# One encoder block on one core: where W_out's upper rows are split, when the second FFN's kept operands are made and loaded, and when norm 2's vectors come

## The chip, the cores and the metric

The kernel runs on one core of a Trainium2 chip, alone. The metric is the time of one execution on the device, in microseconds (us). Five engines work side by side, each through its own instructions in order: PE (matrix products), DVE (elementwise), ACT (elementwise and functions), POOL (elementwise, and it issues DMAs that store) and SP, which issues the DMAs that load.

## The reference

One block with 1024 tokens and a width of 1024, in float32:

```python
x = layer_norm(DN_ALPHA * x + 0.5 * swiglu(x, ffn1_w_gate[l], ffn1_w_up[l], ffn1_w_down[l]), ln1_g[l], ln1_b[l])
z = x @ w_in[l]
fox = forgetting_attention(q, k, v, fg).reshape(bsz, seq, FOX_W)      # 8 heads of 64
u = causal_depthwise_conv(z[..., LX_OFF:LX_OFF + LRU_W], conv_w[l], conv_b[l])
rec = rg_lru(u, rg_wa[l], rg_ba[l], rg_wx[l], rg_bx[l], lru_lambda[l])
lru = jax.nn.gelu(z[..., LG_OFF:LG_OFF + LRU_W]) * rec
mix = jnp.concatenate([fox, lru], axis=-1) @ w_out[l]                 # (1024, 1024) @ (1024, 1024)
x = layer_norm(DN_ALPHA * x + mix, ln2_g[l], ln2_b[l])
x = layer_norm(DN_ALPHA * x + 0.5 * swiglu(x, ffn2_w_gate[l], ffn2_w_up[l], ffn2_w_down[l]), ln3_g[l], ln3_b[l])
```

`swiglu(x, g, u, d)` is `(silu(x @ g) * (x @ u)) @ d` with an inner width of 4096. `layer_norm` is `(x - mean) * rsqrt(var + eps) * g + b` along the 1024 columns.

## The kernel before

**Products.** Every float32 operand is split in two: `hi`, its rounding to a shorter format, cast on ACT, and `lo`, the rest, subtracted on DVE. A product of 128x128 by 128x512 is three matmuls, `hi hi`, `hi lo` and `lo hi` (L163 to L165). Most work on ACT and DVE is this splitting.

**FFN1's first half** (`gate_up`). The 4096 inner columns go in 16 pairs of 256. For each pair the gate and the up matrix, 1024x256 each (1 MB), are loaded raw, and each is multiplied with x by seven block products in place of eight (`one` to `seven`), which take sums and differences of the weights' quarters: L355 makes them on DVE, L349 and L350 split them. `seven` adds into the bank of `six`, and so waits for the copy L659 of it; `three` waits in the same way for L663. The operands of both matrices of a pair, 28 tiles, lie in a pool of 16 buffers (`ws`) that are given out in turn. The first pair of FFN1 (`first_pair`) has an order written out by hand for PE, DVE and ACT, since x has to be transposed and summed there first: L443 copies a transposed block out of its bank, L449 adds two blocks, and L385/L391 split. A scheduler orders all the rest.

**`prepare`** runs beside FFN1's pairs, as a generator: at the steps `two` and `five` of each matrix `next(steps)` does one piece of it. It makes the seven operands of FFN2's first pair ahead, from raw tiles of 128 KB (`aux`, two buffers) that SP loads: a subtraction on DVE, the split (L278 on ACT, L279 on DVE) into a `ws` buffer, and a store to `pre_d` that POOL issues (L285). After 28 such pieces come 16 more, which split rows 0 to 511 of W_out in the same way and store them to `wo_d` (L317).

**Attention.** 64 units, one for each head and tile of 128 queries, run at most three ahead of their use. Up to unit 36 or so the other half of W_out's product fills PE in between. Units 45 to 51 load the four parts of W_out's rows 0 to 511 from `wo_d` (`ready_out_w`, hi and lo of 512 KB each), and units 40, 50 and 52 load the mixed heads that were stored on the way (`mix_d`). Behind the last of them come norm 2's g and b (`load_gb`), and POOL negates g, so that the norm's chain for 1/sqrt(var) can give its negative.

**FFN2's first pair** (`ready_pair`) loads the kept operands from `pre_d`: twelve tiles into `ws` buffers, and t4 and t2 into the two raw buffers (L556); its remaining operands follow later.

Of the kernel before, what the change touches and what calls it, by code (L numbers as in the profile page):

```python
# [59 lines left out]
class Block:  # L60
# [127 lines left out]
    def load_gb(self, g, b, gb):  # L188

        for t, v in zip(gb, (g, b)):  # L190
            self.fetch(t, bass.AP(tensor=v.tensor, offset=v.offset, ap=[[0, P], [1, D]]))
        self.nc.gpsimd.tensor_scalar(gb[0], gb[0], -1.0, 1.0, op0=ALU.mult, op1=ALU.mult)
        self.gb = gb

    def layer_norm(self, i, done=None):
# [67 lines left out]
    def prepare(self, views, to_d, w_out, wsp, ap):  # L263
# [17 lines left out]

        for m, view in enumerate(views):
            for h in range(2):
                def out(n, src):
                    nc.gpsimd.dma_start(to_d[m, OPERANDS.index(n), h], f32(halves(src)))  # L285
# [4 lines left out]
                v.tensor_tensor(b, b, a, ALU.subtract)  # L290
                a = load(view, down, 1)
                yield
                out("t1", b)
                yield
                out("22", a)
                v.tensor_tensor(a, a, b, ALU.subtract)
                b = load(view, down, 0)
                yield
                out("t2", a)
                yield  # L300
                out("21", b)
                v.tensor_tensor(b, b, a, ALU.subtract)
                a = load(view, down, 1)
                yield
                out("t4", b)
                b = load(view, up, 1)
                v.tensor_tensor(a, a, b, ALU.subtract)
                yield
                out("t3", a)
                yield  # L310
        self.wo_d = self.dram.tile([FOX // P, P, 2, D], F32, name="wo_d")
        for f in range(FOX // P):
            for c in range(4):
                cols = slice(c * 2 * P, (c + 1) * 2 * P)
                a = raw()
                nc.sync.dma_start(a.rearrange("p k c -> p (k c)"), w_out[f * P:(f + 1) * P, cols])
                nc.gpsimd.dma_start(self.wo_d[f, :, :, cols], f32(halves(a)).rearrange("p (l k) c -> p l (k c)", l=2))  # L317
                yield
# [15 lines left out]
    def gate_up(self, wg, wu, h_d, rows, bank, tp, wsp, raws=None, later=None, aside=None, ready=None, steps=None):  # L334
# [211 lines left out]
        def ready_pair(g, u):  # L546
# [13 lines left out]
            for n in ("11", "21", "t1"):  # L560
                for m in both:
                    fetch(n, m, two_blocks())
            for n in ("t4", "t2"):
                r = self.rawp.tile([P, 4, 4, P], F32R, tag="raw", name=self.nm("raw"))
                for i, m in enumerate(both):
                    fetch(n, m, (r[:, 2 * i], r[:, 2 * i + 1]))
# [115 lines left out]
        for pair in range(FF // P // 2):  # L682
# [39 lines left out]
            for m in (gate, up):  # L722
# [391 lines left out]
    def ready_out_w(self):  # L1114

        for f in range(FOX // P):
            hl = tuple(self.wsp.tile([P, 4 * VW], F32R, tag="ws", name=self.nm("w"))[:, 0:D] for _ in range(2))
            for l in range(2):
                self.nc.sync.dma_start(f32(hl[l]), self.wo_d[f, :, l])
            yield hl  # L1120

    def attention(self, w_out, mixp, ln, normed):
# [7 lines left out]
        with self.pool("att_p", 3) as pp, self.pool("att_t", 1) as tp, self.pool("att_pt", 6) as ptp, self.pool("att_qk", 2, side="right") as qkp:  # L1130
# [92 lines left out]
            tiles, mix, w_fox, w_steps = [], [], [], self.ready_out_w()  # L1223
# [17 lines left out]
            for n in range(len(units) + AHEAD + 1):  # L1241
# [22 lines left out]
                if 45 <= n < 53 and n % 2:  # L1264
                    w_fox.append(next(w_steps))
                if n in MIXES:
                    mix.append(tuple(self.hp.tile([P, T], F32R, tag="h", name=self.nm("mix")) for _ in range(2)))
                    for l in range(2):
                        nc.sync.dma_start(f32(mix[-1][l]), mix_d[len(mix) - 1][l])
                    if len(mix) == 3:  # L1270
# [144 lines left out]
```

## Time and profile before

| | |
|---|---|
| median of 3 runs | 2322.07 us (2321.42 to 2322.68) |
| the profiled execution, its time | 2323.19 us |
| the profiled execution, its span | 2321.5 us |
| mean granted clock of PE | 0.997 |
| DMA, mean over the span | 139 GB/s |
| read from and written to HBM | 226.81 MB, 94.40 MB |

The trace shows for each instruction its engine, its line, its start and duration, and what ended the idle time ahead of it. In a timeline row the columns are start, duration, engine, line, operation, the tile written, the tiles read, and in brackets the idle time of the engine ahead of it and its releaser. A row of waits has the sum, the number of times and the longest. A row of windows has the stretch and its length; busy time and count of PE, of its weight loads, of DVE, ACT and POOL; the granted clock of PE (1.00 is full speed); the share of the DMA engines; GB/s. Matmuls of 512 columns start 0.23 us apart and are shown 0.39 long, since they overlap.

### The profile page before, as it was taken

To read this page: it belongs to the slowest core of one execution; us is meant where nothing else is said; L and a number is where in the kernel's file an instruction comes from. 1 tells how busy PE (TensorE), PEld (TensorE's weight loads), DVE (VectorE), ACT (ScalarE), POOL (GpSimd) and SP (SyncE) were. 2 spreads that over 40 slices of the span, in tenths; PEclk is the share of its full clock that TensorE was granted. 3 is DMA by queue.
4 is the path that set the end of the run, shared out by engine and by line. 5 is a ranking of instruction groups with operands and counts; after the bars stand their busy time and mean duration, and the time that the engine had idled before them with its cause. 6 is when DMAs were issued, how large, how long until landed. Compare 5 with 4: busy or idle time off the path is not lost.

```text
span 2321.5 us, 28560 instructions
## 1 busy us (share of the span) xinstructions
PE 2298.7 (99%) x10705; PEld 1914.1 (82%) x10705; DVE 1635.6 (70%) x2521; ACT 1019.1 (44%) x1623; POOL 227.8 (10%) x388
## 2 busy tenths in 40 slices
PE   8999999999999999999999999999999999999998
PEld 7888888888888888888898788888888888888887
DVE  7867666666467788866667899565656665577886
ACT  5443434343344345453556755334333333344341
POOL 0121111100000000111133210000000000000000
PEclk9999999999999999999999999999999999999999
DMA  4444444433276433233274934232323232564542
GB/s 150 141 141 145 139 147 141 146 113 125 101 259 234 147 127 109 75 92 110 91 218 126 283 137 141 86 118 89 122 93 123 87 118 87 195 244 168 182 144 73
DMA packets 194444, 323.08 MB, mean 139 GB/s; under 512 B 10033, under 2 KB 115825, under 8 KB 194305
## 3 DMA queue, kind: packets, MB, share of 16 engines
q1 hardware_dynamic: 167712, 230.74, 30.9%
q0 software_dynamic: 26592, 90.51, 9.9%
q8 instruction: 84, 1.38, 0.3%
q14 instruction: 56, 0.45, 0.1%
HBM read 226.81 MB, written 94.40 MB: 138 GB/s over the span
## 4 chain that ended last, share of the span: by engine, by line
PE 81%; issue 10%; DVE 3%; DMA 3%; POOL 2%; ACT 1%; SPq 0%; POOLq 0%; DVEq 0%; ACTq 0%
PE x L163 7%; PE x L164 7%; PE x L165 7%; PE s L165 6%; PE s L164 6%; PE s L163 6%; PE a L165 6%; PE a L164 6%; PE a L163 6%; PE b L163 6%; PE b L164 6%; PE b L165 6%; PE a L1200 1%; PE a L1179 1%; PE a L1049 1%
## 5 line engine op out<-in xcount | busy, mean ns | idle before, releaser
L349 ACT CAST ws<-t 128x512 fp32r<-128x512 f32 x240 | 148.9, 623 | 374.2 <-PE b L164 253.0
L349 ACT CAST ws<-raw 128x512 fp32r<-128x512 f32 x180 | 111.0, 622 | 239.3 <-PE x L164 237.3
L350 DVE TENSOR_TENSOR ws<-t,ws 128x512 fp32r<-128x512 f32 x240 | 164.3, 686 | 56.4 <-ACT ws L349 50.6
L350 DVE TENSOR_TENSOR ws<-raw,ws 128x512 fp32r<-128x512 f32 x180 | 123.3, 688 | 114.4 <-ACT ws L349 110.3
L164 PE MATMUL a<-ws,ws 128*128 128x512 f32 x512 | 199.8, 390 | 0.2
L163 PE MATMUL a<-ws,ws 128*128 128x512 f32 x512 | 199.3, 390 | 0.4 <-ACT row L672 0.4
L163 PE MATMUL b<-As,ws 128*128 128x512 f32 x512 | 199.4, 389 | 0.2 <-ACT row L663 0.2
L164 PE MATMUL b<-As,ws 128*128 128x512 f32 x512 | 199.3, 389 | 0.0
L165 PE MATMUL b<-As,ws 128*128 128x512 f32 x512 | 199.2, 389 | 0.0
L165 PE MATMUL a<-ws,ws 128*128 128x512 f32 x512 | 199.2, 389 | 0.0
L163 PE MATMUL x<-As,ws 128*128 128x512 f32 x504 | 196.6, 390 | 2.1 <-ACT row L659 2.0
L164 PE MATMUL x<-As,ws 128*128 128x512 f32 x504 | 196.1, 389 | 0.0
L165 PE MATMUL x<-As,ws 128*128 128x512 f32 x504 | 196.1, 389 | 0.0
L163 PE MATMUL x<-A,ws 128*128 128x512 f32 x496 | 193.3, 390 | 0.0
L165 PE MATMUL x<-A,ws 128*128 128x512 f32 x496 | 193.0, 389 | 0.0
L164 PE MATMUL x<-A,ws 128*128 128x512 f32 x496 | 193.0, 389 | 0.0
L772 ACT CAST ws<-raw 128x1024 fp32r<-128x1024 f32 x112 | 117.4, 1050 | 157.8 <-PE a L164 87.2
L775 DVE TENSOR_TENSOR ws<-raw,ws 128x1024 fp32r<-128x1024 f32 x112 | 136.6, 1220 | 53.0 <-ACT ws L772 52.6
L702 POOL DMA_DIRECT2D h_d<-row x96 | 68.9, 719 | 968.5 <-DVE row L696 928.4
L163 PE MATMUL s<-ws,ws 128*128 128x512 f32 x384 | 149.5, 389 | 0.0
L165 PE MATMUL s<-ws,ws 128*128 128x512 f32 x384 | 149.4, 389 | 0.0
L164 PE MATMUL s<-ws,ws 128*128 128x512 f32 x384 | 149.4, 389 | 0.0
(295 smaller groups left out, 5252.7 us busy)
## 6 DMA issues: line engine op xcount, KB each, us to landing
raw<-h_d SPq DMA_DIRECT2D x56, 1024.0 KB, 5.4
h_d<-row POOLq DMA_DIRECT2D x96, 512.0 KB, 3.5
wd<-in_ffn_w_down_dram SPq DMA_DIRECT2D x32, 1024.0 KB, 7.5
raw<-in_ffn_w_gate_dram SPq DMA_DIRECT2D x30, 1024.0 KB, 5.3
raw<-in_ffn_w_up_dram SPq DMA_DIRECT2D x30, 1024.0 KB, 5.3
h_d<-row POOLq DMA_DIRECT2D x32, 256.0 KB, 2.7
raw<-in_w_in_dram SPq DMA_DIRECT2D x16, 512.0 KB, 4.9
pre_d<-ws POOLq DMA_DIRECT2D x28, 256.0 KB, 2.7
```

What stands on the lines that cost most here:

```text
L163: mm(out, ah, bh, start=first, stop=False, skip_group_check=goes_on)
L164: mm(out, ah, bl, start=False, stop=False, skip_group_check=goes_on)
L165: mm(out, al, bh, start=False, stop=last, skip_group_check=goes_on)
L349: nc.scalar.copy(hi, src)
L350: v.tensor_tensor(lo, src, f32(hi), ALU.subtract)
L702: nc.gpsimd.dma_start(d[:, 2 * n:2 * n + 2], t.rearrange("p (r t) -> p r t", r=2))
L772: cast = nc.scalar.copy(hi, src)
L775: self.mark = v.tensor_tensor(lo, src, f32(hi), ALU.subtract)
L1049: nc.tensor.matmul(pa[:, 0:width], xh, wh[:, 0:width], start=k == 0, stop=False)
L1179: nc.tensor.transpose(pa[:, (j % 4) * P:(j % 4 + 1) * P], p[:, j * P:(j + 1) * P], self.ident)
L1200: mm(pv[:, ps], vt[:, j, :], pts[h, qt][j // 4][l][:, j % 4, ps], start=j == 0 and l == 0, stop=j == last and l == 1)
```

## The change

Rows 0 to 511 of W_out are loaded raw in attention and split there by `out_w`, as its other rows are already; the 16 pieces in `prepare`, `wo_d` and `ready_out_w` are gone. `prepare` advances once in a matrix, at `two`, and its loads are issued behind the newest raw weight load. The loads of FFN2's kept operands at the start of `ready_pair` are issued behind the last load of the mixed heads. Norm 2's g and b are loaded at unit 38. g is not negated any more, in all three norms: the chain has -0.5 for 0.5 and an addition for a subtraction.

```diff
-        self.nc.gpsimd.tensor_scalar(gb[0], gb[0], -1.0, 1.0, op0=ALU.mult, op1=ALU.mult)
...
-        v.tensor_scalar(w, mv[:, 1:2], EPS, 0.5, op0=ALU.add, op1=ALU.mult)
+        v.tensor_scalar(w, mv[:, 1:2], EPS, -0.5, op0=ALU.add, op1=ALU.mult)
...
-        v.scalar_tensor_tensor(y, w, 1.5, y, op0=ALU.subtract, op1=ALU.mult)
+        v.scalar_tensor_tensor(y, w, 1.5, y, op0=ALU.add, op1=ALU.mult)
...
                 a, b = load(view, up, 0), load(view, up, 1)
-                out("11", a)
-                v.tensor_tensor(b, b, a, ALU.subtract)
+                yield
+                keep(m, h, "11", a)
+                less(b, a)
                 a = load(view, down, 1)
                 yield
...
-        self.wo_d = self.dram.tile([FOX // P, P, 2, D], F32, name="wo_d")
-        for f in range(FOX // P):
-            for c in range(4):
-                cols = slice(c * 2 * P, (c + 1) * 2 * P)
-                a = raw()
-                nc.sync.dma_start(a.rearrange("p k c -> p (k c)"), w_out[f * P:(f + 1) * P, cols])
-                nc.gpsimd.dma_start(self.wo_d[f, :, :, cols], f32(halves(a)).rearrange("p (l k) c -> p l (k c)", l=2))
-                yield
...
-            nc.sync.dma_start(r, view[:, :, pair * 2 * P:(pair + 1) * 2 * P])
+            self.weight_load = nc.sync.dma_start(r, view[:, :, pair * 2 * P:(pair + 1) * 2 * P])
...
+            with self.tc.issue_after(self.mix_load.ins):
+                for n in ("11", "21", "t1"):
+                    for m in both:
+                        fetch(n, m, two_blocks())
...
-                    if steps and step in ("two", "five"):
-                        next(steps, None)
+                    if steps and step == "two":
+                        with self.tc.issue_after(self.weight_load.ins):
+                            next(steps, None)
...
-            tiles, mix, w_fox, w_steps = [], [], [], self.ready_out_w()
+            tiles, mix, w_fox, w_steps = [], [], [], self.out_w(w_out, 0)
...
+                if n == 38:
+                    self.load_gb(*ln, [self.hp.tile([P, T], F32, tag="h", name=self.nm("gb")) for _ in range(2)])
```

The scheduler places what these lines say. Line numbers of the change are up to twelve lower than those of before.

DVE in FFN1's first pair, before (L290 is the subtraction of `prepare`, L391 splits, L355 makes t1 and t2, L449 adds two transposed blocks):

```order
L355 TENSOR_TENSOR t_264<-raw_136 128x512
L391 TENSOR_TENSOR ws_176<-raw_135,ws_175 128x512
L391 TENSOR_TENSOR ws_178<-raw_136,ws_177 128x512
L290 TENSOR_TENSOR aux_775<-aux_775,aux_773 128x256
L391 TENSOR_TENSOR ws_180<-t_261,ws_179 128x512
L355 TENSOR_TENSOR t_289<-raw_135,t_261 128x512
L391 TENSOR_TENSOR ws_182<-t_264,ws_181 128x512
L355 TENSOR_TENSOR t_292<-raw_136,t_264 128x512
L449 TENSOR_TENSOR ws_280<-b_300,ws_183 128x512
```

and in the change, at the same place (L385, L349 and L443 are those three):

```order
L349 TENSOR_TENSOR t_264<-raw_136 128x512
L385 TENSOR_TENSOR ws_176<-raw_135,ws_175 128x512
L385 TENSOR_TENSOR ws_178<-raw_136,ws_177 128x512
L385 TENSOR_TENSOR ws_180<-t_261,ws_179 128x512
L349 TENSOR_TENSOR t_289<-raw_135,t_261 128x512
L385 TENSOR_TENSOR ws_182<-t_264,ws_181 128x512
L349 TENSOR_TENSOR t_292<-raw_136,t_264 128x512
L443 TENSOR_TENSOR ws_280<-b_300,ws_183 128x512
```

The subtraction of the aux tiles has left the first pair; it stands in pair 1.

ACT in one of FFN1's later pairs, before (L278 casts `prepare`'s tiles, here W_out's; L659 is the copy that `seven` waits for):

```order
L278 CAST ws_3596<-aux_3594 128x256
L278 CAST ws_3629<-aux_3627 128x256
L653 COPY row_3464<-x_3659 128x512
L672 COPY row_3460<-x_3542 128x512
L278 CAST ws_3704<-aux_3702 128x256
L676 ACTIVATE row_3460<-row_3460 128x1024
L278 CAST ws_3737<-aux_3735 128x256
L349 CAST ws_3775<-raw_3773 128x512
L349 CAST ws_3779<-raw_3773 128x512
L349 CAST ws_3787<-t_3785 128x512
L349 CAST ws_3791<-t_3783 128x512
L659 COPY row_3462<-x_3659 128x512
```

and in the change, in a later pair (L277 and L654 are those two):

```order
L277 CAST ws_3773<-aux_3290 128x256
L648 COPY row_3643<-x_3832 128x512
L667 COPY row_3639<-x_3721 128x512
L277 CAST ws_3876<-aux_3584 128x256
L671 ACTIVATE row_3639<-row_3639 128x1024
L343 CAST ws_3945<-raw_3943 128x512
L343 CAST ws_3949<-raw_3943 128x512
L343 CAST ws_3957<-t_3955 128x512
L343 CAST ws_3961<-t_3953 128x512
L654 COPY row_3641<-x_3832 128x512
```

Of four casts of `prepare` ahead of the copy two are left, and these keep operands of FFN2's first pair.

DVE in attention, at the end of the fourth head, before (L1164 adds the bias to the scores and takes the minimum, L1184 splits the transposed weights, L1204 adds to a head's output):

```order
L1164 ISA p_11038,m_11042<-s_11035,cum_10527 128x128
L1164 ISA m_11042 128x1
L1184 TENSOR_TENSOR pt_11012<-a_11013,pt_11011 128x4x128
L1204 TENSOR_TENSOR o_10773<-o_10773,a_11020 64x256
L1164 ISA p_11058,m_11062<-s_11053,cum_10825 128x1024
L1164 ISA m_11062 128x1
L1184 TENSOR_TENSOR pt_11012<-a_11045,pt_11011 128x3x128
L1184 TENSOR_TENSOR pt_11066<-a_11067,pt_11065 128x2x128
L1164 ISA p_11092,m_11096<-s_11087,cum_10825 128x896
L1164 ISA m_11096 128x1
L1184 TENSOR_TENSOR pt_11066<-a_11099,pt_11065 128x128
```

and in the change (L1152, L1172 and L1192 are those three; L156 is the subtraction of a split of W_out):

```order
L1152 ISA p_10944,m_10948<-s_10941,cum_10429 128x128
L1152 ISA m_10948 128x1
L156 TENSOR_TENSOR w_11299<-raw_11296,w_11298 128x1024
L1172 TENSOR_TENSOR pt_10914<-a_10915,pt_10913 128x4x128
L1192 TENSOR_TENSOR o_10675<-o_10675,a_10922 64x256
L1172 TENSOR_TENSOR pt_10914<-a_10951,pt_10913 128x3x128
L1152 ISA p_10964,m_10968<-s_10959,cum_10727 128x1024
L1152 ISA m_10968 128x1
L1172 TENSOR_TENSOR pt_10972<-a_10973,pt_10971 128x2x128
L1152 ISA p_10998,m_11002<-s_10993,cum_10727 128x896
L1152 ISA m_11002 128x1
L156 TENSOR_TENSOR w_11377<-raw_11296,w_11376 128x1024
```

Two of the four subtractions stand in this piece; the other two are some ten rows ahead of it.

More of the change, by code (lines that the diff above doesn't have):

```diff
@@ L261, in block_1, with prepare @@
         return lambda: self.nc.scalar.copy(unsplit(rows, half), pt)
-    def prepare(self, views, to_d, w_out, wsp, ap):
+    def prepare(self, views, to_d, wsp, ap):
         nc, v = self.nc, self.nc.vector
@@ L280, in halves, with keep, less @@
             return t
+        def keep(m, h, n, src):
+            nc.gpsimd.dma_start(to_d[m, OPERANDS.index(n), h], f32(halves(src)))
+        def less(x, y):
+            v.tensor_tensor(x, x, y, ALU.subtract)
         for m, view in enumerate(views):
             for h in range(2):
[L284 to L285 removed]
                 up, down = 2 * h, 4 + 2 * h
                 a, b = load(view, up, 0), load(view, up, 1)
[L289 to L290 removed]
+                yield
+                keep(m, h, "11", a)
+                less(b, a)
                 a = load(view, down, 1)
                 yield
[L293 removed]
+                keep(m, h, "t1", b)
                 yield
[L295 to L296 removed]
+                keep(m, h, "22", a)
+                less(a, b)
                 b = load(view, down, 0)
                 yield
[L299 removed]
+                keep(m, h, "t2", a)
                 yield
[L301 to L302 removed]
+                keep(m, h, "21", b)
+                less(b, a)
                 a = load(view, down, 1)
                 yield
[L305 removed]
+                keep(m, h, "t4", b)
                 b = load(view, up, 1)
[L307 removed]
                 yield
[L309 to L318 removed]
+                less(a, b)
+                keep(m, h, "t3", a)
     def gu_views(self, *ws):
@@ L558, in fetch @@
                 m.w[n] = to
[L560 to L566, printed above, removed]
+            with self.tc.issue_after(self.mix_load.ins):
+                for n in ("11", "21", "t1"):
+                    for m in both:
+                        fetch(n, m, two_blocks())
+                for n in ("t4", "t2"):
+                    r = self.rawp.tile([P, 4, 4, P], F32R, tag="raw", name=self.nm("raw"))
+                    for i, m in enumerate(both):
+                        fetch(n, m, (r[:, 2 * i], r[:, 2 * i + 1]))
             t21 = [block() for _ in range(4)]
@@ L1112, in out_w @@
                 yield tuple(t[:, 0, :] for t in self.split_ws(r[:, j:j + 1, :], 1))
[L1114 to L1120, printed above, removed]
     def attention(self, w_out, mixp, ln, normed):
@@ L1268, in attention @@
                     for l in range(2):
-                        nc.sync.dma_start(f32(mix[-1][l]), mix_d[len(mix) - 1][l])
-                    if len(mix) == 3:
-                        self.load_gb(*ln, [self.hp.tile([P, T], F32, tag="h", name=self.nm("gb")) for _ in range(2)])
+                        self.mix_load = nc.sync.dma_start(f32(mix[-1][l]), mix_d[len(mix) - 1][l])
                 if tiles:
@@ L1316 @@
             nc.sync.dma_start(rows[i], xf[i * P:(i + 1) * P, :])
-        steps = blk.prepare(blk.gu_views(ffn2_w_gate[0], ffn2_w_up[0]), pre_d, w_out[0], wsp, ap)
+        steps = blk.prepare(blk.gu_views(ffn2_w_gate[0], ffn2_w_up[0]), pre_d, wsp, ap)
         finish = blk.gate_up(ffn1_w_gate[0], ffn1_w_up[0], h_d[0], rows, bank, tp, wsp, raws, open_s4, lambda: blk.mixer_consts(
```

## The prediction, made before the changed kernel ran

> **What bounds the kernel now.** I read the page first, then PE's part of the waits, then the timeline of PE, ACT and DVE around the longest of these waits, and last the windows of attention's end. PE does nearly all of the time:
>
> ```profile
> PE 2298.7 (99%) x10705; PEld 1914.1 (82%) x10705; DVE 1635.6 (70%) x2521; ACT 1019.1 (44%) x1623; POOL 227.8 (10%) x388
> ...
> PE b L163 <- ACT ws L443: 2.8, 1, 2.8
> PE s L1158 <- DVE m L1164: 2.4, 7, 0.9
> PE x L163 <- ACT row L659: 2.0, 3, 1.2
> ```
>
> The span is 2321.5 us, so PE idles 22.8 us in all, and the change leaves PE's work as it is: no matmul is added or dropped. Only PE's stops can move, and those above are the largest three: one in FFN1's first pair (2.8), three in FFN1's later pairs (2.0), seven in attention (2.4). The start, up to PE's first product, and the norm behind the last matmul are not touched.
>
> **The first pair: what is removed.** PE transposes four row tiles and then stops:
>
> ```profile
> 17.73 3.66 PE L249 MATMUL b<-ident,x 128*128 128x128 f32 x32
> 24.19 0.50 PE L163 MATMUL b<-A,ws 128*128 128x512 f32 x1 [2.80 <-ACT ws L443]
> ...
> 19.33 0.60 ACT L443 COPY ws<-b 128x512 f32<-128x512 f32 x1
> 23.04 0.62 ACT L385 CAST As<-ws 128x512 fp32r<-128x512 f32 x1 [3.11 <-DVE ws L449]
> 23.56 0.58 ACT L443 COPY ws<-b 128x512 f32<-128x512 f32 x1
> ...
> 15.62 1.29 DVE L391 TENSOR_TENSOR ws<-raw,ws 128x512 fp32r<-128x512 f32 x2
> 19.57 0.43 DVE L290 TENSOR_TENSOR aux<-aux,aux 128x256 f32<-128x256 f32 x1 [2.66 <-DMA aux<-in_ffn_w_gate_dram]
> 22.32 1.28 DVE L449 TENSOR_TENSOR ws<-b,ws 128x512 f32<-128x512 f32 x2
> ```
>
> Read it backwards. PE at 24.19 waits for a bank that ACT's third L443 empties at 23.56; ACT could not get to it, since the cast ahead waits for DVE's first L449 (22.32); and DVE stood 2.66 us before L290, the one `prepare` instruction that the scheduler had put into this pair, which needs an aux load issued behind all the opening loads. In the change the aux loads stand behind pair 1's raw loads and that subtraction in pair 1 (the rows of DVE's order above). So DVE goes on at 16.91 instead of 19.91, 3.0 us earlier (the wait and 0.34 of L290): L449 at 19.3, the cast at 20.0, the third L443 at 20.5 to 21.1. PE's transposes last to 21.39: the 2.80 are gone, and nothing that I see is late there next.
>
> Behind the stop PE runs at half speed for a while:
>
> ```profile
> 25.71 0.63 PE L163 MATMUL b<-A,ws 128*128 128x512 f32 x1
> 26.14 0.63 PE L164 MATMUL b<-A,ws 128*128 128x512 f32 x1
> ...
> 29.08 0.39 PE L165 MATMUL b<-A,ws 128*128 128x512 f32 x1
> 29.31 0.40 PE L163 MATMUL b<-A,ws 128*128 128x512 f32 x1
> ...
> 20.00:30.00 10.00, 7.20 (x31) 5.80 (x30) 9.47 (x16) 5.19 (x10) 0.00 (x0) 0.83 0.01 2
> 40.00:50.00 10.00, 10.00 (x48) 8.31 (x47) 9.75 (x17) 7.10 (x13) 0.00 (x0) 1.00 0.01 2
> 50.00:60.00 10.00, 9.96 (x50) 7.93 (x49) 9.91 (x17) 6.24 (x9) 0.00 (x0) 1.00 0.63 210
> ```
>
> Starts are 0.43 us apart instead of 0.23: eight such steps between 25.71 and 29.08 cost (29.08 - 25.71) - 8 x 0.23 = 1.5 us, with a granted clock of 0.83 in that window and 1.00 in the later ones. It follows the only long stop after PE got going, so I let it go with the stop. PE would gain 2.8 + 1.5 = 4.3, and some 0.2 for its restart.
>
> The Trainium skill says otherwise of that drop: "TensorE: Matmul & The Clock Gate", section "Part 1: The HAM clock gate", has the clock halved only after at least one idle window of about 3.4 us. The stop here was 2.80 us, so by that rule it isn't the cause, and the 1.5 us would stay. The trace has both within 2 us of each other and no second case; this is a rival below.
>
> What DVE allows: it is 9.75 and 9.91 of 10 busy from 40 to 60, so PE can only come earlier by what DVE gains. That is 3.0, and its waits for PE in between, which go when PE is ahead by more than DVE is:
>
> ```profile
> 28.51 0.69 DVE L436 TENSOR_TENSOR row<-b,row 128x512 f32<-128x512 f32 x1 [0.35 <-PE b L165]
> 31.56 0.69 DVE L436 TENSOR_TENSOR row<-b,row 128x512 f32<-128x512 f32 x1 [0.56 <-PE b L165]
> 38.34 0.69 DVE L475 TENSOR_TENSOR ws<-ws,b 128x512 f32<-128x512 f32 x1 [0.42 <-PE b L249]
> ```
>
> 3.0 + 0.35 + 0.56 + 0.42 = 4.3, the same as PE's. The subtraction comes back in pair 1, while DVE is still full there: 0.3 lost. **Term: -4.0**; bounds -2.7 (DVE's 3.0 less the 0.3) and -4.5.
>
> **FFN1's later pairs.** The three stops of 2.0 us all end with L659, the copy that `seven` waits for. By starts they cost more than the idle time that is shown:
>
> ```profile
> 169.07 0.39 PE L165 MATMUL b<-As,ws 128*128 128x512 f32 x1
> 170.67 0.50 PE L163 MATMUL x<-As,ws 128*128 128x512 f32 x1 [1.22 <-ACT row L659]
> ...
> 399.44 0.39 PE L165 MATMUL b<-As,ws 128*128 128x512 f32 x1
> 400.03 0.50 PE L163 MATMUL x<-As,ws 128*128 128x512 f32 x1 [0.20 <-ACT row L659]
> ...
> 438.05 0.39 PE L165 MATMUL b<-As,ws 128*128 128x512 f32 x1
> 438.99 0.50 PE L163 MATMUL x<-As,ws 128*128 128x512 f32 x1 [0.55 <-ACT row L659]
> ...
> 396.05 0.62 ACT L349 CAST ws<-t 128x512 fp32r<-128x512 f32 x1 [1.10 <-DMA wo_d<-ws]
> 398.87 0.62 ACT L349 CAST ws<-t 128x512 fp32r<-128x512 f32 x1 [2.19 <-DMA wo_d<-ws]
> ```
>
> 1.60, 0.59 and 0.94, each less the normal 0.23: 1.37 + 0.36 + 0.71 = 2.4, and about 0.1 for each restart (the first matmul behind a stop takes 0.50 instead of 0.39): 2.8. The ACT rows show why: a cast ahead of L659 wants a ws buffer that a store of `prepare` still reads. A pair makes four such stores close together; the change makes two, half a pair apart, and none for W_out. In the stop at 399 the two waits are 3.3 us for a stop of 0.4, so ACT has 2.9 us in hand once they are gone, and one wait of 1.1 would still be covered. The pairs behind the eleventh, which had no steps, get two each: a cast and a subtraction, in that slack. **Term: -2.8**; bounds -1.6 (the 0.36 and half of the first stop stay, the half that two table loads and other waits may make) and -3.2 (smaller stops go as well).
>
> **Attention: what is added.** Four casts on ACT and four subtractions on DVE of a kind that the trace has:
>
> ```profile
> L155 ACT CAST w<-raw x20: 1037/1054/1057, 924.3 to 1184.8; 128x1024 fp32r<-128x1024 f32 x20
> L156 DVE TENSOR_TENSOR w<-raw,w x20: 1171/1224/1227, 925.3 to 1185.9; 128x1024 fp32r<-128x1024 f32 x20
> ...
> w<-wo_d SPq DMA_DIRECT2D x8, 512.0 KB, 10.3
> ...
> 1280.00:1290.00 10.00, 10.00 (x60) 8.52 (x59) 8.40 (x19) 6.40 (x15) 2.28 (x6) 1.00 0.64 165
> 1290.00:1300.00 10.00, 9.98 (x72) 8.87 (x71) 7.88 (x20) 7.26 (x20) 1.17 (x4) 1.00 1.01 349
> 1300.00:1310.00 10.00, 9.21 (x67) 7.70 (x65) 8.75 (x26) 9.03 (x22) 2.40 (x8) 1.00 1.04 263
> 1320.00:1330.00 10.00, 8.11 (x55) 6.56 (x54) 8.21 (x18) 7.41 (x18) 3.26 (x8) 1.00 1.03 365
> ```
>
> 4 x 1.05 = 4.2 us of ACT and 4 x 1.22 = 4.9 of DVE. The order puts them at the fourth head's end and the fifth's start, 1287 to 1302 in this trace. There PE's filling work ends and PE begins to stop (0.8 of 10 us, then 1.9), with DVE 79 to 88% busy. DVE has 1.6 + 2.1 + 1.3 us free in these 30 us: it can take most of the 4.9, but not at its place. Laid into the rows one by one, the first two splits fall into gaps, and the last two, at the fifth head's end, push DVE back by about 1.0. Bounds: -0.5 and +4.9. Below nothing, since the 4 MB in which W_out's parts were loaded (8 x 512 KB), while the DMA engines are 1.01 to 1.04 busy, become 2 MB loaded a hundred us earlier. I take the value nearest to the rows laid in. **Term: +1.0.**
>
> **What costs nothing.** The kept operands in the raw buffers (t4, t2) are loaded behind the last mix load instead of early in attention, where W_out's raw rows take their place, and have time:
>
> ```profile
> 1334.77 0.42 SPq L105 DMA_DIRECT2D gb<-in_ln_b_dram  x1
> 1370.01 45.65 SPq L556 DMA_DIRECT2D ws<-pre_d  x20
> ...
> 1414.83 0.39 PE L163 MATMUL b<-A,raw 128*128 128x512 f32 x1
> ```
>
> SP has nothing between 1335 and 1370; eight loads with 80 us to go cost nothing unless a raw buffer came free some 60 us late. Norm 2's vectors take SP's time ahead of the first mix load, where W_out's first parts stood beside it. Without the negation POOL drops three instructions, and the norm has as many as before.
>
> **The sum.** -4.0 - 2.8 + 1.0 = -5.8 us. The profiled execution took 2323.19 (its span and 1.7 around it), 1.1 over the median of 2322.07; it becomes 2317.4, and the median **2316.3**.
>
> **The rivals.**
> - *The splits take the place of the stops.* DVE passes all of its 4.9 on to PE, as it would where every unit waits for the one before: PE's seven waits for DVE's m (2.4) speak for it, the gaps in DVE against it. -6.8 + 4.9 = -1.9: 2320.2.
> - *A wait takes the first stop's place.* If PE's banks or the ACT copies hold it at 21.4 for as long as DVE gained too little, 1 us of the 4.0 is left: 2319.3. Against it: L443 would be done before PE's transposes are.
> - *The clock drop stays*: it comes with this place in the program, with the work before the stop, and not with the stop. 2316.3 + 1.5 = 2317.8. Against it: no window between 30 and 60 shows a second one. That the stop is too short to be the cause is what the Trainium skill's page on the clock gate would say.
> - *The change doesn't do what it says*: were the scheduler's new places for the two subtractions of pair 1 as bad (DVE waiting 2.66 for an aux load there), the first term would be nought: 2320.3.
> - *Slower.* Each split holds PE for cast and subtraction, 1.05 + 1.22 = 2.3, four times 9.1, and two of these stops slow the clock as at 25 us, 1.5 each: 12.1 - 6.8 = +5.3: 2327.4. It decides from 11.4 us lost in attention on (the 6.8 and 0.2%). It needs raw rows that are not there or an ACT without gaps; ACT is 64 and 73% busy there.
>
> **How the numbers follow.** Two runs of this kernel differ by up to 1.3 us, and 0.2% (4.6 us) is about what a measurement can tell from no change: faster means under 2317.4. My forecast has 0.66, the splits in place of the stops 0.12, the wait in the first stop's place 0.07, the clock drop 0.05, the change without effect in the opening 0.05, slower 0.05. The forecast's lower end is all three terms at their good bounds, -4.5 - 3.2 - 0.5 = -8.2: 2313.9; its upper end, two terms half way to their bad ones, 2318.3. The range is 2313.6 to 2320.3: it takes in the splits and the lost stop, and leaves out the slower case and the tails. Of the forecast four fifths lie under 2317.4, 0.53, and some of the clock's case, 0.02: faster 0.55, slower 0.05, same 0.40.
>
> **What would show it.** PE's wait on L443 gone, and a granted clock of 1.00 from 20 to 30; PE's `x L163 <- ACT row L659` under 0.6; no `wo_d`; PE's waits in 1290 to 1340 up by about 1. I am wrong if PE idles longer from 50 to 75 than the 0.4 of now, if the first pair keeps a stop of over 1 us, or if attention's end grows by more than 3.

## The result, and the profile after

| | before | changed |
|---|---|---|
| median of 8 runs | 2321.94 us (2321.29 to 2322.68) | 2315.44 us (2313.87 to 2316.95) |
| ratio, with its 95% interval | | 0.9972 (0.9962 to 0.9983) |
| the profiled execution, its time | 2323.19 us | 2315.55 us |
| the profiled execution, its span | 2321.5 us | 2313.8 us |
| read from and written to HBM | 226.81 MB, 94.40 MB | 222.61 MB, 90.21 MB |

The change makes the kernel 6.5 us faster by the medians, and by its interval something between 3.9 and 8.8. Measured a second time, beside other runs of before, the same kernel had 2315.46 against 2322.87, with the same ratio. The two profiled executions lie 7.6 apart.

First the first line of the page of the changed kernel, then PE's part of its waits (sum, number of times, longest):

```profile
PE 2295.7 (99%) x10705; PEld 1912.3 (83%) x10705; DVE 1634.9 (71%) x2509; ACT 1017.2 (44%) x1611; POOL 214.2 (9%) x369
```

```profile
PE b L248 <- DMA row<-in_x_dram: 2.3, 3, 1.5
PE s L1146 <- DVE m L1152: 1.6, 6, 0.4
PE b L1299 <- POOL ident masks.py:199: 1.4, 1, 1.4
PE a L1188 <- ACT pt L1171: 0.9, 3, 0.4
```

Two of the three largest movable waits of before are gone from the list: that for L443 (2.8) and that of `x L163` for L659 (2.0). The third, for DVE's m in attention, is 1.6 in place of 2.4. No other single wait is longer than 0.5 us, but for those of the start.

The opening of the changed kernel, from the timelines of PE, ACT and DVE (L248 transposes, L437 is before's L443, L443 its L449), and the windows:

```profile
18.07 3.66 PE L248 MATMUL b<-ident,x 128*128 128x128 f32 x32
21.89 0.49 PE L163 MATMUL b<-A,ws 128*128 128x512 f32 x1 [0.16 <-ACT ws L437]
22.23 0.40 PE L164 MATMUL b<-A,ws 128*128 128x512 f32 x1
...
21.26 0.58 ACT L437 COPY ws<-b 128x512 f32<-128x512 f32 x1
...
16.40 1.30 DVE L385 TENSOR_TENSOR ws<-raw,ws 128x512 fp32r<-128x512 f32 x2
17.60 0.69 DVE L385 TENSOR_TENSOR ws<-t,ws 128x512 fp32r<-128x512 f32 x1
...
20.01 1.29 DVE L443 TENSOR_TENSOR ws<-b,ws 128x512 f32<-128x512 f32 x2
...
20.00:30.00 10.00, 9.84 (x52) 8.20 (x51) 9.82 (x17) 5.91 (x12) 0.00 (x0) 1.00 0.01 2
1290.00:1300.00 10.00, 8.93 (x56) 6.75 (x54) 9.44 (x20) 8.08 (x19) 2.35 (x5) 1.00 1.04 264
1300.00:1310.00 10.00, 9.69 (x73) 8.54 (x72) 8.95 (x26) 7.47 (x21) 3.66 (x11) 1.00 0.97 270
1310.00:1320.00 10.00, 9.48 (x69) 8.08 (x67) 8.63 (x21) 9.12 (x21) 4.39 (x10) 1.00 0.65 193
1320.00:1330.00 10.00, 9.40 (x65) 8.16 (x65) 8.50 (x22) 7.95 (x19) 2.16 (x7) 1.00 0.88 300
```

DVE goes from L385 to L385 without a gap, the copy L437 ends at 21.84, and PE stands 0.16 us where it stood 2.80. The granted clock from 20 to 30 is 1.00 in place of 0.83. In attention the loss has moved to an earlier place: from 1290 to 1300 PE is busy for 8.93 in place of 9.98, and from 1320 to 1330 for 9.40 in place of 8.11 (at the same time the changed kernel is some 7 us further on in the program, so the windows are compared by their pattern alone).

**Where the time went.** Both kernels issue 10705 matmuls, in the same order but for some 70 of them in attention, between 1298 and 1343 us. So the start of the nth matmul in one profile can be set against the start of the nth in another; this difference, PE's place, says at each point of the program how far ahead PE is. Its growth over a stage is what the stage brought (minus: gained against before's profile, in us; times are before's; a place between 1298 and 1343 can be off by some tenths, since the order differs there):

| | opening, 20 to 30 | FFN1, 100 to 640 | attention, 1280 to 1350 |
|---|---|---|---|
| predicted | -4.0 | -2.8 | +1.0 |
| changed kernel | -4.2 | -3.2 | -0.6 |
| the same again | -4.7 | -2.9 | -0.4 |

The three stages of the changed kernel come to -8.0; outside of them its profile is 0.3 behind before's, all of it already there at 20 us, so that 7.7 are left of the span.

### The profile page after: what moved, and what is told of

It reads as the page before. It is cut to its first block, busy times and chain, and to the rows that moved or that the text cites. A ratio compares the mean times of both kernels' runs of the same rounds, so it can differ in the third digit from the quotient of the medians.

```text
span 2313.8 us, 28429 instructions
## 1 busy us (share of the span) xinstructions
PE 2295.7 (99%) x10705; PEld 1912.3 (83%) x10705; DVE 1634.9 (71%) x2509; ACT 1017.2 (44%) x1611; POOL 214.2 (9%) x369
## 3 DMA queue, kind: packets, MB, share of 16 engines
HBM read 222.61 MB, written 90.21 MB: 135 GB/s over the span
## 4 chain that ended last, share of the span: by engine, by line
PE 94%; DVE 3%; ACT 1%; issue 1%; DMA 0%; SPq 0%; DVEq 0%; ACTq 0%
PE x L163 10%; PE x L165 10%; PE x L164 10%; PE b L163 8%; PE b L164 8%; PE b L165 8%; PE s L165 6%; PE s L164 6%; PE s L163 6%; PE a L163 6%; PE a L164 6%; PE a L165 6%; PE a L1188 1%; PE a L1167 1%; PE a L1045 1%; PE a L1047 1%
## 5 line engine op out<-in xcount | busy, mean ns | idle before, releaser
L163 PE MATMUL a<-ws,ws 128*128 128x512 f32 x512 | 199.3, 390 | 0.4 <-ACT row L667 0.4
L163 PE MATMUL b<-As,ws 128*128 128x512 f32 x512 | 199.4, 389 | 0.2 <-ACT row L658 0.2
L163 PE MATMUL x<-As,ws 128*128 128x512 f32 x504 | 196.2, 389 | 0.0
L163 PE MATMUL x<-A,ws 128*128 128x512 f32 x496 | 193.3, 390 | 0.1
L163 PE MATMUL s<-ws,ws 128*128 128x512 f32 x384 | 149.5, 389 | 0.0
```

The costliest lines, as they stand in the source:

```text
L163: mm(out, ah, bh, start=first, stop=False, skip_group_check=goes_on)
```

## The experiments

### The tie alone

The kernel before, with the steps tied behind the raw loads and nothing else:

```diff
-            nc.sync.dma_start(r, view[:, :, pair * 2 * P:(pair + 1) * 2 * P])
+            self.weight_load = nc.sync.dma_start(r, view[:, :, pair * 2 * P:(pair + 1) * 2 * P])
...
                     if steps and step in ("two", "five"):
-                        next(steps, None)
+                        with self.tc.issue_after(self.weight_load.ins):
+                            next(steps, None)
```

> The kernel before with one edit: prepare's step, and so its aux loads, tied behind the raw weight loads of its pair; still two steps for each matrix, W_out still prepared in FFN1. The built order has the subtraction L290 in pair 1 instead of the first pair, all else of the opening as before. Theory (the subtraction held DVE for an aux load, and the half clock behind the stop follows from the stop): PE is 3.9 us earlier at 30 us, granted clock 1.00 from 20 to 30; the stops of FFN1's later pairs (before L659 at 169, 247, 399, 438) all stay; span and time 4.0 less than before, 3.5 to 4.6. Rival, the half clock belongs to the place in the program: 2.4 less, the steps of 0.43 us stay. Rival, it takes one step a matrix or the added yield as well: within 0.5 of before.

Measured: 2318.39 against 2322.84, ratio 0.9984 (0.9976 to 0.9993). PE's place moves by -4.7 from 20 to 30 us. FFN1 neither gains nor loses (0.0): PE's wait for L659 is 2.3 us in three, where before had 2.0 in three. The windows of this run:

```profile
20.00:30.00 10.00, 10.00 (x55) 8.53 (x54) 9.75 (x17) 6.35 (x13) 0.00 (x0) 1.00 0.01 2
```

PE has no idle time from 20 to 30 and a full clock. The whole of the opening's gain is in one place of one subtraction, and the half speed goes with the stop. Not as expected: of the four stops by starts that at 438 did not come, while those at 247 and 399 grew (0.25 to 0.80 and 0.36 to 0.79); the sum is 2.8 where before has 2.7. So the tie moves the stops within FFN1 and does not shorten them.

### The change without the tie

```diff
-                        with self.tc.issue_after(self.weight_load.ins):
-                            next(steps, None)
+                        next(steps, None)
```

> The changed kernel without the tie of prepare's steps to the raw loads. In the built order nothing else moves: the first two aux loads stand two places earlier on SP, and the one subtraction is back in the first pair on DVE. Theory: DVE waits 2.5 to 3 us before it, PE stops 2.8 us for ACT's copy and, where most of that stop lies in one 3.41 us stretch of the clock, runs at half speed for the next: PE's place at 30 us 3.9 to 4.7 later than in the change, time 3 to 5 above the change's, FFN1's later pairs and attention as in the change (within 0.4). Rival, the drop of the clock is chance: only 2.5 to 3.0 later at 30 us. Rival, the aux loads come two places earlier and so in time: within 1.

Measured: 2320.72 against 2322.56, ratio 0.9989 (0.9980 to 0.9998). Against its own runs of before it gains 1.8, where the changed kernel gained 6.5; PE's place falls 6.1 behind the changed kernel's from 20 to 30 us. From the timelines of PE and DVE (L285 is the subtraction), and the windows cut where the granted clock can change:

```profile
24.43 0.80 PE L163 MATMUL b<-A,ws 128*128 128x512 f32 x1 [3.80 <-ACT ws L437]
25.02 0.63 PE L164 MATMUL b<-A,ws 128*128 128x512 f32 x1
25.45 0.63 PE L165 MATMUL b<-A,ws 128*128 128x512 f32 x1
...
19.80 0.43 DVE L285 TENSOR_TENSOR aux<-aux,aux 128x256 f32<-128x256 f32 x1 [3.21 <-DMA aux<-in_ffn_w_gate_dram]
...
16.07:19.48 3.41, 3.41 (x28) 3.20 (x27) 0.52 (x1) 1.94 (x4) 0.00 (x0) 1.00 0.95 358
19.48:22.90 3.42, 1.15 (x11) 0.91 (x9) 3.10 (x6) 0.00 (x0) 0.00 (x0) 1.00 0.02 5
22.90:26.31 3.41, 1.88 (x5) 1.50 (x6) 3.32 (x6) 2.63 (x5) 0.00 (x0) 0.50 0.00 0
26.31:29.72 3.41, 3.41 (x10) 2.64 (x9) 1.99 (x4) 2.57 (x5) 0.00 (x0) 0.50 0.00 0
29.72:33.14 3.42, 3.42 (x16) 2.82 (x15) 2.93 (x5) 0.00 (x0) 0.00 (x0) 1.00 0.00 0
```

With the added `yield` and one step a matrix the subtraction is back in the first pair all the same; it is the tie that keeps it out. The stop is 3.8 here, 1.0 longer than in before, and two stretches in a row run at half speed. PE works for 1.88 us of the first of them, which costs another 0.9. Together that is why the loss is 6.1 and not 3.9 to 4.7: the expectation counted a stop of 2.8 and one slow stretch. In before the same view shows one:

```profile
18.78:22.19 3.41, 2.61 (x24) 2.37 (x22) 2.62 (x5) 1.15 (x3) 0.00 (x0) 1.00 0.07 19
22.19:25.61 3.42, 1.42 (x6) 1.21 (x7) 3.33 (x7) 2.57 (x5) 0.00 (x0) 1.00 0.00 0
25.61:29.02 3.41, 3.41 (x9) 2.68 (x9) 2.97 (x5) 2.62 (x6) 0.00 (x0) 0.50 0.00 0
29.02:32.43 3.41, 3.41 (x16) 2.80 (x16) 2.85 (x6) 0.00 (x0) 0.00 (x0) 1.00 0.00 0
```

PE was idle for 2.0 of the 3.42 us from 22.19 to 25.61, and the next stretch is the slow one.

### Stops of other lengths

To see when a stop costs the clock, the changed kernel with ACT's copy in front of `seven` repeated 6 to 18 times more, in the gate matrix of FFN1's pairs 3 to 15; the added copies are work that the kernel does not need:

```diff
-                nc.scalar.copy(m.u, m.product("t2", "s2", m.sum))
+                x = m.product("t2", "s2", m.sum)
+                for _ in range(1 + m.extra):
+                    nc.scalar.copy(m.u, x)
...
+                m.extra = pair + 3 if steps and m is gate and pair > 2 else 0
```

> The changed kernel with ACT's copy of six's bank (in front of seven) repeated 6 to 18 times more, in the gate matrix of FFN1's pairs 3 to 15, so that PE stops there for a growing time: some 1 to 8 us, read from the trace. Theory (the half clock follows from the stop itself, once PE idles for well over half of one of the 3.41 us stretches in which the granted clock changes): stops of 2.5 us and more are followed by starts 0.43 us apart, for about 3.4 us and 1.5 to 1.7 us lost, wherever they lie; stops under 1.5 us are not; between, it depends on whether the stop lies in one stretch. Rival, the clock is halved only behind a stop that covers a whole such stretch, 3.4 us and more: then none behind stops of 2 to 3.4 us, and the opening's drop had another cause, such as the transposes ahead of it.

One execution, 2329.51. The added copies cost PE 11.9 us in FFN1 against the changed kernel's profile, two thirds of it in stops of under 0.4. One stop of over 2 us came out, at 548 us. It does not stand in front of `seven`: PE waits for a bank that DVE empties (L663), DVE's split ahead of that waits for a cast on ACT, and the cast for a buffer that a store of `prepare` still reads. From the timelines of PE and ACT, and the windows:

```profile
550.65 0.50 PE L163 MATMUL x<-A,ws 128*128 128x512 f32 x1 [2.37 <-DVE row L663]
...
548.65 1.14 ACT L343 CAST ws<-raw 128x512 fp32r<-128x512 f32 x2 [4.48 <-DMA pre_d<-ws]
...
546.16:549.57 3.41, 2.12 (x10) 1.43 (x8) 0.27 (x1) 0.92 (x2) 0.00 (x0) 1.00 0.23 88
549.57:552.99 3.42, 2.34 (x10) 1.97 (x11) 2.35 (x5) 2.27 (x4) 0.00 (x0) 1.00 0.00 0
552.99:556.40 3.41, 3.41 (x16) 2.83 (x16) 2.04 (x4) 2.83 (x5) 0.00 (x0) 1.00 0.00 0
```

The stop is a little shorter than before's (2.37 against 2.80), and 1.29 of it lie in one stretch and 1.08 in the next. The clock stays at 1.00. Whether that is for the length or for the place, this one stop does not tell. The same with 17 to 29 repeats was to bring longer ones:

> The run with repeated copies once more, with 17 to 29 repeats instead of 6 to 18, since only one stop of over 2 us came of those: 2.53 us, 1.45 of it in one 3.41 us stretch of the clock and 1.07 in the next, and no drop behind it. Theory (a stretch with PE idle for over half of it, 1.7 us, is followed by one at half speed): each stop that puts over 1.8 us into one stretch is followed by starts 0.43 us apart in the next, each that puts under 1.6 into both is not. Rival, only a stretch that is idle as a whole does it: no drop behind stops under 3.4 us, whatever their place.

It did not (one execution, 2327.04): the longest stop before `seven` was 0.6 us, and no stretch behind the opening ran at half speed while PE worked. So both expectations stay undecided, and whether a stop of over 2.4 us slows the clock elsewhere than in the opening stays untested.

### W_out's way alone

The kernel before, with `out_w` in attention, the steps for `wo_d` deleted and the kept operands fetched behind the last mix load:

```diff
-        self.wo_d = self.dram.tile([FOX // P, P, 2, D], F32, name="wo_d")
...
-            tiles, mix, w_fox, w_steps = [], [], [], self.ready_out_w()
+            tiles, mix, w_fox, w_steps = [], [], [], self.out_w(w_out, 0)
...
+            with self.tc.issue_after(self.mix_load.ins):
```

> The kernel before with W_out's rows 0 to 511 split in attention and no wo_d steps in FFN1; the kept operands fetched behind the last mix load; opening, four steps a pair, g's negation and norm 2's vectors as before. Theory (stores of prepare hold the ws buffers that the casts ahead of L659 want): the stops at 399 and 438, where W_out's steps were, go (1.1 us by starts, with restarts 1.3), those at 24, 169 and 247 stay. In attention the prediction had 1.0 lost: then the time is 0.1 to 0.3 below before. The change's trace has 0.5 gained from 1290 to 1350: then it is 1.6 to 1.8 below. Rival, the gain at attention's end belongs to norm 2's vectors and not to W_out's way: no more than 1.3 below before in all, and PE at 1350 no earlier against its place at 1280.

Measured: 2323.40 against 2322.84, ratio 1.0000 (0.9991 to 1.0009). FFN1 gains 1.6, and the stops at 399 and 438 are gone. Attention loses 2.0, more than either expectation had. The chain of it, from the timelines of SP, POOL, DVE and PE:

```profile
1285.06 11.44 SPq L1262 DMA_DIRECT2D mix<-mix_d  x4
...
1300.66 0.52 SPq L1136 DMA_DIRECT2D cum<-cum_d  x1
...
1310.40 0.54 POOL L1155 TENSOR_SCALAR_AFFINE_SELECT cum<-cum 128x128 f32<-128x128 f32 x2 [4.30 <-DMA cum<-cum_d]
...
1310.97 0.42 DVE L1157 CUSTOM_DVE_ANT_0 p<-s,cum 128x256 f32<-128x256 f32 x1 [2.59 <-POOL cum L1155]
...
1311.46 0.50 PE L1151 MATMUL s<-kh,q 128*128 128x512 f32 x1 [2.37 <-DVE m L1157]
```

Two of the mix loads wait for a store of mixed heads that has not landed, and the seventh head's loads stand behind them in SP's queue (the expectations count heads from 0: their sixth and seventh are the seventh and eighth). Its bias row (`cum`) is issued at 1300.66 and lands 9.6 us later. POOL waits for it with an instruction for the seventh head, and behind that stands the one for the sixth head's last units, which DVE and through it PE wait for.

### W_out's way with norm 2's vectors at unit 38

The run before this one, with one edit more:

```diff
+                if n == 38:
+                    self.load_gb(*ln, [self.hp.tile([P, T], F32, tag="h", name=self.nm("gb")) for _ in range(2)])
...
-                    if len(mix) == 3:
-                        self.load_gb(*ln, [self.hp.tile([P, T], F32, tag="h", name=self.nm("gb")) for _ in range(2)])
```

> The run with W_out split in attention (opening, FFN1's steps and g's negation as before) with one edit more: norm 2's vectors loaded at unit 38. In the built order of SP the second pair of mix loads then stands behind the sixth head's loads and not ahead of them, where it waited 7.7 us for a store of mixed heads. Theory (the splits themselves cost nothing that PE sees; what cost 2.0 us in attention there was the sixth head's bias row, which came late behind those mix loads): no wait of DVE for POOL's bias over 0.5 us, attention (PE's place at 1350 less that at 1280) within 0.4 of the changed kernel's profile, and the time 1.4 to 2.4 below before, that is FFN1's part alone. Rival, the splits cost 1 to 2 us and single profiles differ by as much: attention 1 to 2 us longer than before, time 0.0 to 0.9 below before.

Measured: 2320.37 against 2322.87, ratio 0.9992 (0.9984 to 1.0001). FFN1 -1.5, attention -0.6, and DVE's wait for the bias row is 0.6 in two where it was 2.7 in two; POOL's instruction for the seventh head waits 0.85 us for the row in place of 4.30. In SP's timeline:

```profile
1287.11 0.93 SPq L1264 DMA_DIRECT2D mix<-mix_d  x2
...
1297.65 0.53 SPq L1136 DMA_DIRECT2D cum<-cum_d  x1
...
1303.28 1.01 SPq L1264 DMA_DIRECT2D mix<-mix_d  x2
```

The bias row goes ahead of the second two mix loads, which have stopped nobody. The vectors take two buffers of the pool that the mixed heads are loaded into, and the later mix loads move back. In before the vectors are late too, but there the second two mix loads stand behind `wo_d` loads and the loads of the seventh and eighth heads in SP's order, and so stop neither of the two bias rows.

### The change with the vectors where they were

The reverse: the changed kernel with g and b behind the last mix load and g negated on POOL.

> The changed kernel with norm 2's vectors loaded behind the last mix load again and g negated on POOL, norm's signs as before; all else as in the change. Theory (these edits cost and bring nothing, since SP and POOL have room): within 0.3 of the change's time, PE's places from 1280 to 1350 within 0.3. Rival, the 0.5 us that the change gained from 1290 to 1350 come from the vectors' early load, which clears SP and the DMA engines for the mix loads: 0.5 to 1.5 above the change, lost between 1300 and 1350.

Measured: 2316.99 against 2322.84, ratio 0.9977 (0.9968 to 0.9985); against the changed kernel's 0.9972 that is no difference to be told. In attention its profile is 0.4 slower than the change's, lost between 1300 and 1310 (behind that it gains 0.2 and loses them again): SP holds four mix loads for 11.27 us, and the bias row is issued at 1295.09 in place of 1291.17. POOL waits 2.12 us for it, where it waits 0.84 in the change. The program in attention is the same as in the run of W_out's way alone, instruction for instruction, and yet that one lost 2.0. So with the vectors late the row comes so late that the execution decides how much is lost: 0.4 and 2.6 us against the change's profile in the two that there are. The 0.4 alone is no more than profiles of the change's attention differ by.

### The vectors alone

The kernel before with the vectors at unit 38, W_out from `wo_d`:

> The kernel before with one edit: norm 2's vectors at unit 38 (g still negated), W_out's upper rows loaded from wo_d as before. The built order of DVE and ACT in attention stays as before; on SP the second mix loads move behind the sixth head's. It tells from what the changed kernel's attention, 0.5 us shorter from 1280 to 1350 than before's though it has four splits more, is shorter. Theory (the four splits shift the scheduler's places, so that DVE's score minimum at the seventh head's start no longer stands behind a sum that waits for ACT; the vectors alone bring nothing without them): from 1320 to 1335 PE loses as much as in before, attention within 0.4 of before's, time within 0.8 of before. Rival, the vectors' early place relieves the loads there with or without the splits: attention 1 to 2 us shorter than before, time 0.8 to 2 less.

Measured: 2324.14 against 2322.77, ratio 1.0005 (0.9996 to 1.0014); attention 1.0 longer than in before's profile. The rival falls: by themselves the vectors bring nothing. But attention is longer than the theory's 0.4 allows, too; where the 0.9 from 1280 to 1300 in the table below come from stays open. The vectors matter only once W_out's `wo_d` loads no longer stand between the mix loads.

Attention in parts, from PE's places (us; minus is gained against before's profile):

| | 1280 to 1300 | 1300 to 1320 | 1320 to 1350 | sum |
|---|---|---|---|---|
| changed kernel | +1.3 | 0.0 | -1.8 | -0.6 |
| the same again | +1.3 | -0.2 | -1.5 | -0.4 |
| W_out and vectors | +1.3 | 0.0 | -1.8 | -0.6 |
| W_out, vectors late | +1.2 | +2.3 | -1.6 | +2.0 |
| change, vectors late | +1.2 | +0.2 | -1.6 | -0.2 |
| tie alone (attention as before) | 0.0 | -0.5 | -0.3 | -0.7 |
| vectors alone | +0.9 | -0.3 | +0.4 | +1.0 |

The splits cost 1.2 to 1.3 us where they stand, and every kernel that has them gains 1.5 to 1.8 some 30 us later. DVE's timeline at the eighth head's start shows a reason, first in before, with the PE row that waits, then in the change:

```profile
1325.48 0.41 DVE L1204 TENSOR_TENSOR o<-o,a 64x256 f32<-64x256 f32 x1 [0.64 <-ACT o L1203]
1325.82 1.21 DVE L1164 CUSTOM_DVE_ANT_0 p<-s,cum 128x1024 f32<-128x1024 f32 x1
...
1327.09 0.50 PE L1158 MATMUL s<-kh,q 128*128 128x512 f32 x1 [0.93 <-DVE m L1164]
```

```profile
1316.72 1.22 DVE L1152 CUSTOM_DVE_ANT_0 p<-s,cum 128x1024 f32<-128x1024 f32 x1
...
1319.64 0.41 DVE L1192 TENSOR_TENSOR o<-o,a 64x256 f32<-64x256 f32 x1 [0.77 <-ACT o L1191]
...
1318.88 0.48 PE L1146 MATMUL s<-kh,q 128*128 128x512 f32 x1
```

In before the minimum over 1024 scores, which PE needs, stands behind a sum that waits for ACT; with the splits the scheduler has put it ahead, and PE's matmul does not wait. Whether this turn alone brings the 1.5 to 1.8, or also the 4 MB of `wo_d` loads that go from there, no run separates.

### The same kernel again

> The changed kernel itself once more, as a measure of how much a single profile's stages differ between executions. Theory (attention's length with the splits is steady once the sixth head's loads go ahead of the mix loads): PE's place at each of 30, 450, 1280 and 1350 us within 1.0 of the first profile and the differences between these places within 0.3; time 5.5 to 7.5 below before. Rival, attention's length changes from one execution to the next by 1 to 2 us.

Measured: 2315.46 against 2322.87, ratio 0.9972 (0.9961 to 0.9984). PE's places at 30, 450, 1280 and 1350 are 0.5, 0.2, 0.1 and 0.1 from those of the first profile. Attention is within 0.1, the opening's gain 0.5 more, FFN1's 0.3 less: a stop of 0.24 at 165 us, which the first profile does not have.

### Prepare's steps

Three runs vary FFN1. The first is the changed kernel with two steps a matrix:

```diff
-                    if steps and step == "two":
+                    if steps and step in ("two", "five"):
```

> The changed kernel with two steps a matrix instead of one, so that prepare's 28 pieces go four to a pair as before and end by pair 7; ties and attention as in the change. Theory (the stores of four pieces a pair hold ws buffers): PE stops before L659 near 165 and 242 come back, 1.4 and 0.4 by starts; time 1.6 to 2.0 above the change's. Rival, what stopped PE there was the place of the aux loads or the table loads, which the tie moved: within 0.4 of the change. In between, 0.4 to 1.2, each has a part of it.

Measured: 2316.79 against 2322.84, ratio 0.9976 (0.9966 to 0.9986). One stop comes back, 0.40 at 164 us, where the theory had two of 1.4 and 0.4; FFN1 is 0.7 behind the change's profile, between the theory and the rival. The second takes the tie away as well:

> The changed kernel with two steps a matrix and without the tie: against the kernel before, prepare's new order of pieces and no W_out in FFN1, with four pieces a pair. FFN1's stops before seven from 100 to 450 us, by starts and with restarts, were 3.1 us in before, 1.6 without W_out (old order, no tie), 0.6 with new order and tie at four pieces a pair, 0.1 in the change. Theory (the order of a piece's subtraction and store matters, the tie doesn't): 0.4 to 0.8. Rival, the tie brought it: 1.4 to 1.8. In the opening the stop and the half speed come back, 3.9 to 4.7 us later at 30 us than in the change.

One execution, 2320.98. FFN1 is at -2.4 against before (-2.5 with the tie), so the tie has no part there; in the opening PE falls 5.3 behind the run with the tie, more than the expectation had. The third is the changed kernel with the steps from pair 2 on:

```diff
-                    if steps and step == "two":
+                    if steps and step == "two" and pair > 1:
```

> The changed kernel with prepare's steps from pair 2 on instead of pair 1 (28 pieces in the 28 places that are left). DVE has no gap from 30 to 70 us there, and PE stops at 53 and 70 us for 0.3 and 0.5 with restarts. Theory (the subtraction and two splits that stand on DVE in pair 1 set these stops): they shrink, 0.3 to 0.8 less than the change. Rival, the stops belong to the first pairs' own splits: within 0.2 of the change's profile at 100 us, and the time the same; or a step in the last pair runs into FFN1's down product, then up to 1 us more.

Measured: 2316.28 against 2322.56, ratio 0.9973 (0.9962 to 0.9983), the same as the change. The stops at 52 and 69 us stay to within 0.02 us, so they belong to the first pairs' own work; and a stop of 0.94 stands at 164, so that FFN1 brings 2.0 in this profile and not 3.2. No version was found that beats the changed kernel.

## Why the prediction was right, and where not

- **The stop in the first pair**, -4.0 with bounds of -2.7 and -4.5. Right in its mechanism and its size: -4.2, -4.7 again, and -4.7 with the tie alone. DVE's wait went, and nothing came late next but 0.16 us of the same copy. The upper bound was 0.2 short. How much there is to gain differs between executions: in the two runs with the change's steps and no tie, DVE waited 3.2 for the aux load in place of 2.66, the stop was 3.8, and the opening was 1.0 and 1.9 longer than in before's profile. The prediction's sizes rest on the one profile it had.
- **The half speed goes with the stop.** Right: from 20 to 30 us the clock is 1.00 in all eight profiles without the stop, and all six with it have a slow stretch there. The rival that the drop belongs to the place falls. What the prediction took from the Trainium skill, "TensorE: Matmul & The Clock Gate", section "Part 1: The HAM clock gate", that it takes an idle window of 3.4 us, does not hold here: no stretch of the opening was idle as a whole, and 2.0 idle of 3.42 were enough.
- **The tie, not the new order of the pieces,** moves the subtraction. The prediction put it on the aux loads' new place; the run without the tie shows that the rest of the change would not have done it.
- **FFN1's later pairs**, -2.8 with bounds of -1.6 and -3.2. Right: -3.2 and -2.9. By parts: without W_out's steps -1.6 and -1.5; the new order of pieces about 0.9 more (-2.5 and -2.4, two profiles); half as many steps a pair 0.2 to 0.8 more (-2.8 to -3.2 in four profiles). The prediction laid all of it on the number of stores in a pair. The order inside a piece it did not mention, and it has at least as large a part as the number of steps. The last part is no larger than what profiles of the same steps differ by (a stop at 165 us of 0.00, 0.24 and 0.17), and is not shown.
- **Attention**, +1.0 with bounds of -0.5 and +4.9. The step that failed is laying the splits into the rows of before one by one. Up to 1300 it held: 1.2 to 1.3 lost where the splits stand, and 1.0 was put there. But it took all that follows as unchanged. The order behind the splits is another one, and 30 us later it gave the loss back. The sum is -0.6 to 0.0 in the seven profiles with the change's attention and FFN1 without added copies (+0.6 and -0.3 in the two with them), and 0.0 to -0.7 in the two profiles of before's own: no difference. PE's idle time from 1290 to 1340, which was named as a sign and was to rise by about 1, is 2.5 in place of 3.5, though the two windows do not hold quite the same matmuls. That the two parts cancel was not foreseen.
- **What costs nothing.** For the kept operands right: SP issues them behind the last mix load, and PE never waits. For norm 2's vectors the step failed. They were said to take SP's time and no more; without their early place attention is 0.4 and 2.6 us longer in the two profiles there are, through a bias row behind two mix loads. What the change leaves out (`wo_d` between the mix loads) brings a new wait (DVE waits 2.7 us in two for POOL's bias there, 0.5 in two in before), and the vectors keep it short (0.6 in two).
- **The sum.** -5.8 forecast; -6.5 by the medians, -7.6 between the profiles. Against the -8.0 of the three stages the rest is attention's +1.0, which did not come (1.6), and some 0.6 of the two terms of FFN1 and the opening, about what profiles of one kernel differ by. So the time lies this near to the forecast with one of its three terms wrong.

## What to carry to other kernels

An operation off the path that a scheduler hoists into an ordered stretch makes its engine wait for whatever that operation loads; tie the load behind the loads that the stretch itself needs, and look at the built order to see that the operation has left. Where a queue of loads is in program order, a load that waits for a store holds back all that stand behind it: before taking transfers out from between two loads, see what then moves up. A piece added to a stage that a scheduler orders is not paid for at its place alone; compare places of the same instruction well behind it.

## What was not expected of the hardware

The granted clock changes in stretches of 3.41 us: in every profile here it changes only at whole multiples of 3.413 us from its first record, and where the stretches begin differs from one execution to the next. A stretch at half speed follows one in which PE stood idle for a good part:

| run, stretch | idle, of 3.4 us | the next stretch |
|---|---|---|
| without the tie, 19.48 to 22.90 | 2.27 | half |
| before, 22.19 to 25.61 | 2.00 | half |
| without the tie, 22.90 to 26.31 (itself at half speed) | 1.53 | half |
| the vectors alone, 2312.22 to 2315.64 (PE's last products) | 1.82 | full |
| W_out's way alone, 1307.45 to 1310.86 | 1.77 | full |
| before, 1326.09 to 1329.50 | 1.47 | full |
| repeated copies, 546.16 to 549.57 | 1.29 | full |
| repeated copies, 549.57 to 552.99 | 1.08 | full |
| the first transposes: the same kernel again, 5.50 to 8.91 | 1.66 | half |
| the first transposes: the tie alone, 5.16 to 8.57 | 1.52 | half |
| the first transposes: two steps and no tie, 4.73 to 8.14 | 1.54 | full |

The rows for attention, in before and in the run of W_out's way alone, from the windows:

```profile
1326.09:1329.50 3.41, 1.94 (x13) 1.43 (x13) 3.36 (x8) 2.82 (x5) 0.58 (x2) 1.00 1.03 354
1329.50:1332.92 3.42, 3.42 (x28) 3.16 (x27) 2.08 (x5) 3.31 (x9) 0.69 (x2) 1.00 0.99 404
```

```profile
1307.45:1310.86 3.41, 1.64 (x14) 1.27 (x12) 0.90 (x4) 1.71 (x5) 0.46 (x2) 1.00 1.09 312
1310.86:1314.28 3.42, 2.82 (x20) 2.63 (x21) 2.64 (x10) 2.05 (x7) 1.46 (x4) 1.00 1.02 216
```

From a stretch at full speed, and behind the first microseconds, the bound lies between 1.82 and 2.00 us idle of 3.41. In the first microseconds it does not: 1.52 was followed by half speed and 1.54 by full, so idle time as the windows show it is not all that counts there, and why is open. Behind the first microseconds the length of the single stop would divide the cases as well: the six stops that a slow stretch followed are 2.80 to 3.81 us long, and the two longest that none followed are 2.37 (at 548 us above, and at 1309 us in the run of W_out's way alone). No run sets the two apart there; in the first microseconds a slow stretch came without any stop of over 1 us (the same kernel again). A slow stretch costs 1.5 us where PE works through it, as in before from 25.61 to 29.02. If it is the idle time in one stretch that counts, a stop of 2.5 us costs 2.5 or 4.0, by where it falls in the stretches; that is an estimate, and no run has such a stop.
